# The first load of a streaming weighted sum: one DMA of 52 KB rows, and the last weights in three DMAs

## The chip, the core and the metric

The kernel runs on one core of one Trainium2 chip. The metric is device time in microseconds (us) of one execution. Before the change it is 238.91 us, the median of 3 runs (238.84 to 239.22).

## What is computed

For each of 16 x 1024 tokens there are two expert outputs of 512 floats and two weights. The result is their weighted sum.

```
batch, seq, hidden, k = 16, 1024, 512, 2
weights = combine_weights[..., np.newaxis]             # (16, 1024, 2, 1)
out = np.sum(expert_outputs * weights, axis=2)         # (16, 1024, 2, 512) -> (16, 1024, 512), float32
```

The input is 67 MB and the output is 33.5 MB. Two multiplications and one addition are done for each output element.

## The kernel before, in words

The 16384 tokens are dealt over 128 partitions, 128 tokens to each (`per`). The first 115 of a partition (`main`) lie together in memory, and the last 13 (`LAST`) lie together in a second region. A token is 4 KB of input (2 x 512 floats) and 2 KB of output. A partition's tokens are cut into ten tiles of 13, 13, 12, 13, 13, 13, 12, 13, 13 and 13 tokens (`TILES`), numbered 0 to 9. The buffer `et` has four rooms of 13, 13, 12 and 13 tokens, and tile g lives in room g mod 4. All weights fit in one buffer, `wt`.

`load` (line 76) moves a whole tile by one DMA on the queue of SyncE (SP in the profile, q1 among the DMA queues). Each partition's part of a tile is one row of the DMA: 13 tokens are 52 KB. Tile 0 is the exception: `FIRST` (line 33) splits it into a load of 2 tokens and one of 11, and line 119 tells the first that a row may not be longer than 4 KB, so it has 256 rows. Then come the loads of tiles 1, 2 and 3.

Ahead of the loads in the program, on the queue of ScalarE (ACT in the profile, q10 among the DMA queues), stand: a small store of zeros `zt` into places of the output that are written over later (line 111), the weights of the first 115 tokens of each partition (line 112, one DMA, 128 rows of 920 B), and those of the last 13 tokens in two DMAs of 64 partitions each (lines 113 and 114, rows of 104 B). The two engines issue side by side.

After that a loop runs over the stores (`STORES`). For tiles 0 to 7 `combine` does one multiplication of the whole tile by the weights on VectorE (DVE in the profile, line 88), in place, and one addition of the halves (line 97). Tile 8 shares its work with ACT (lines 92, 94, 96 and 97). Tile 9 goes token by token over ACT and DVE (lines 102 and 103). Its weights are the ones loaded last. The result lies in the tile's own room, and line 130 stores it: tiles 0 to 6 one at a time from ACT's queue, tiles 7 and 8 in one store and tile 9 in another from SP's queue. After the store of tile g, SP issues the load of tile g + 4 into the same room, which must wait until that store has landed. The program's order is the order on each engine's queue (`manual_schedule`); the waits between them are put in by the framework from what each instruction reads and writes. The framework also gives each DMA one of a few completion semaphores in turn, and a DMA that reuses one waits for the transfer that had it before.

Of the kernel before, what the change touches and what calls it, by code (L numbers as in the profile page):

```python
# [1 line left out]

# [4 lines left out]


@with_exitstack
def kernel(  # L10
    ctx: ExitStack,
    tc: tile.TileContext,
    expert_outputs: bass.AP,
    combine_weights: bass.AP,
    out: bass.AP,
):

    nc = tc.nc
    b, s, k, h = expert_outputs.shape
    assert k == 2
    n = b * s
    P = nc.NUM_PARTITIONS
    per = n // P
    assert per * P == n

    ROOM = [13, 13, 12, 13]
    ROOMS = len(ROOM)  # L30
    SITE = [sum(ROOM[:i]) for i in range(ROOMS)]
    TILES = [13, 13, 12, 13, 13, 13, 12, 13, 13, 13]
    FIRST = [2, 11, 13, 12, 13]
    STORES = [[0], [1], [2], [3], [4], [5], [6], [7, 8], [9]]
    WHOLE = [0, 1, 2, 3, 4, 5, 6, 7]
    MIXED = [8]
    ALONE = 3
    FREE = {9: 0}
    LAST = 13
    assert all(c <= ROOM[g % ROOMS] for g, c in enumerate(TILES))  # L40
    assert sum(TILES) == per and [g for st in STORES for g in st] == list(range(len(TILES)))
    main = per - LAST
    starts = [sum(TILES[:g]) for g in range(len(TILES))]

    def rows(x):

        first = x[0 : P * main, :].rearrange("(p t) f -> p t f", p=P)
        second = x[P * main : n, :].rearrange("(p t) f -> p t f", p=P)
        return lambda t, c: first[:, t : t + c, :] if t < main else second[:, t - main : t - main + c, :]

    flat = out.rearrange("b s h -> (b s) h")
    eo = rows(expert_outputs.rearrange("b s k h -> (b s) (k h)"))
    cw = rows(combine_weights.rearrange("b s k -> (b s) k"))
    o = rows(flat)

    dt = mybir.dt.float32
    mult = mybir.AluOpType.mult
    add = mybir.AluOpType.add
    copy = mybir.ActivationFunctionType.Copy

    pool = ctx.enter_context(tc.tile_pool(name="all", bufs=1))
    et = pool.tile([P, sum(ROOM), k * h], dt)
    halves = et.rearrange("p j (k h) -> p (j k) h", k=k)
    wt = pool.tile([P, per * k], dt)
    wk = wt.rearrange("p (t k) -> p t k", k=k)
    zt = pool.tile([16, 128], dt)
    warm = pool.tile([P, 1], dt)

    def place(t):
        g = max(g for g in range(len(TILES)) if starts[g] <= t)  # L70
        return SITE[g % ROOMS] + t - starts[g]

    def load(t, c, **kw):
        at = place(t)
        assert place(t + c - 1) == at + c - 1
        nc.sync.dma_start(out=et[:, at : at + c], in_=eo(t, c), **kw)  # L76

    def weights(q, t, c):
        q.dma_start(out=wk[:, t : t + c, :], in_=cw(t, c))

    def combine(g, base):
        at, c, t0 = SITE[g % ROOMS], TILES[g], starts[g]
        if g in WHOLE or g in MIXED:
            room = halves[:, k * at : k * (at + c), :]
            x0, x1 = et[:, at : at + c, 0:h], et[:, at : at + c, h : 2 * h]
            if g in WHOLE:
                wb = wt[:, k * t0 : k * (t0 + c)].unsqueeze(2).to_broadcast([P, k * c, h])
                nc.vector.tensor_tensor(out=room, in0=room, in1=wb, op=mult)  # L88
            else:
                for i in range(ALONE, c):  # L90
                    x = et[:, at + i, 0:h]
                    nc.scalar.activation(out=x, in_=x, func=copy, scale=wt[:, k * (t0 + i) : k * (t0 + i) + 1])  # L92
                w1 = wk[:, t0 : t0 + c, 1:2].to_broadcast([P, c, h])
                nc.vector.tensor_tensor(out=x1, in0=x1, in1=w1, op=mult)  # L94
                w0 = wk[:, t0 : t0 + ALONE, 0:1].to_broadcast([P, ALONE, h])
                nc.vector.tensor_tensor(out=x0[:, 0:ALONE], in0=x0[:, 0:ALONE], in1=w0, op=mult)  # L96
            nc.vector.tensor_tensor(out=halves[:, base : base + c, :], in0=x0, in1=x1, op=add)  # L97
            return
        for i in range(c):
            t = k * (t0 + i)  # L100
            x0, x1 = halves[:, k * (at + i), :], halves[:, k * (at + i) + 1, :]
            nc.scalar.activation(out=x0, in_=x0, func=copy, scale=wt[:, t : t + 1])  # L102
            nc.vector.scalar_tensor_tensor(  # L103
                out=halves[:, base + i, :], in0=x1, scalar=wt[:, t + 1 : t + 2], in1=x0, op0=mult, op1=add
            )

    with tc.manual_schedule():
        nc.vector.memset(zt, 0.0)  # L108

        ahead = flat[0 : P * main, :].rearrange("(q t) h -> q (t h)", q=16)  # L110
        nc.scalar.dma_start(out=ahead[:, 0:128], in_=zt)  # L111
        weights(nc.scalar, 0, main)
        for half in (slice(0, P // 2), slice(P // 2, P)):
            nc.scalar.dma_start(out=wk[half, main:per, :], in_=cw(main, per - main)[half])
        nc.scalar.activation(out=warm, in_=nc.const_aps.tensor(1.0, (P, 1), dt), func=copy)  # L115

        t = 0
        for i, c in enumerate(FIRST):
            load(t, c, **({"max_dma_last_dim": k * h * 4} if i == 0 else {}))
            t += c  # L120
        assert t == sum(TILES[:ROOMS])
        for j, st in enumerate(STORES):
            room = FREE.get(st[0], st[0] % ROOMS)
            base, c = SITE[room] * k, 0
            for g in st:
                combine(g, base + c)
                c += TILES[g]
            assert c <= k * ROOM[room]
            q = nc.sync if j in (7, 8) else nc.scalar
            q.dma_start(out=o(starts[st[0]], c), in_=halves[:, base : base + c, :])  # L130
            for g in st:
                if g + ROOMS < len(TILES):
                    load(starts[g + ROOMS], TILES[g + ROOMS])


# [1 line left out]
_INS = ['expert_outputs', 'combine_weights']  # L137
_OUTS = [((16, 1024, 512), 'float32')]


# [23 lines left out]
```

## Time and profile before

| | |
|---|---|
| median of 3 runs | 238.91 us |
| the profiled execution's own time | 238.91 us |
| its span, first to last instruction | 237.1 us |
| DVE busy | 190.0 us (80% of the span), 33 instructions |
| ACT busy | 15.8 us (7%), 25 instructions |
| DMA | 100.80 MB in 3344 packets, 425 GB/s over the span |
| first 2 tokens of tile 0, from issue to landing | 5.0 us |
| other 11 tokens of tile 0 | 18.2 us |
| weights of the first 115 tokens | 18.2 us |
| weights of the last 13 tokens | 31.0 us (median of two DMAs) |
| first multiplication on DVE starts at | 19.73 us |

How to read it: the span is cut at the first and the last instruction, and what lies outside it is part of the time alone. Instructions that issue DMAs are not counted as busy; they are listed with the time from issue to landing. In the view of DMA queues a packet is one row of a DMA, or a completion mark of 4 B, and the shares are those of the 16 DMA engines' time. In the timeline the bracket behind an instruction is the idle time of its engine ahead of it and what ended it.

### The profile page before, as it was taken

What the parts mean: (1) busy time and instruction counts of PE and PEld (TensorE: products, weight loads), DVE (VectorE), ACT (ScalarE), POOL (GpSimd) and SP (SyncE); (2) the same over time, 40 slices, a digit from 0 to 9 for tenths busy, and PEclk for the clock granted to TensorE, in tenths of its full rate; (3) what the DMA queues carried; (4) which work ended last, traced back from release to release, by engine and by line L of the source; (5) the groups of instructions that cost most, each with busy time, mean ns of one, the idle gap of its engine ahead of it and who ended that gap; (6) DMA issues with size and microseconds to landing.
All of it is one profiled execution on the core that took longest, in us unless ns stands there. A gap on an engine that the chain in (4) does not pass through costs nothing.

```text
span 237.1 us, 154 instructions
## 1 busy us (share of the span) xinstructions
DVE 190.0 (80%) x33; ACT 15.8 (7%) x25; POOL 0.2 (0%) x4
## 2 busy tenths in 40 slices
DVE  0006999999999999999999998998499969919400
ACT  2000000000000000000000000000000055019200
POOL 0000000000000000000000000000000000000000
DMA  8999999989999999999899999999899999899996
GB/s 300 388 481 434 432 421 398 470 348 485 449 431 458 431 440 390 486 420 420 359 492 409 409 509 392 431 503 431 359 431 503 420 397 483 381 431 431 431 431 287
DMA packets 3344, 100.80 MB, mean 425 GB/s; under 512 B 512, under 2 KB 656, under 8 KB 912
## 3 DMA queue, kind: packets, MB, share of 16 engines
q1 hardware_dynamic: 2000, 77.33, 75.9%
q10 hardware_dynamic: 1344, 23.47, 23.0%
HBM read 67.24 MB, written 33.56 MB: 425 GB/s over the span
## 4 chain that ended last, share of the span: by engine, by line
DVE 55%; DMA 36%; issue 1%; ACT 0%; DVEq 0%; ACTq 0%; SPq 0%
DVE et L88 35%; DVE et L97 17%; DMA out_dram<-et 17%; DMA et<-in_expert_outputs_dram 12%; DMA wt<-in_combine_weights_dram 8%; DVE et L103 3%; ACT et L102 0%; DVEq L159 0%; ACTq L111 0%; DVE zt L108 0%; DVEq L88 0%; SPq L76 0%; ACTq L102 0%
## 5 line engine op out<-in xcount | busy, mean ns | idle before, releaser
L88 DVE TENSOR_TENSOR et<-et,wt 128x13312 f32<-128x13312 f32 (+1 forms) x8 | 110.0, 13754 | 23.8 <-DMA wt<-in_combine_weights_dram 18.7
L97 DVE TENSOR_TENSOR et<-et 128x6656 f32<-128x6656 f32 (+1 forms) x9 | 62.8, 6973 | 0.4
L92 ACT ACTIVATE et<-et,wt 128x512 f32<-128x512 f32 x10 | 6.2, 708 | 188.0 <-DMA et<-in_expert_outputs_dram 188.0
L103 DVE SCALAR_TENSOR_TENSOR et<-et,wt 128x512 f32<-128x512 f32 x13 | 8.7, 747 | 5.0 <-ACT et L102 5.0
L102 ACT ACTIVATE et<-et,wt 128x512 f32<-128x512 f32 x13 | 8.1, 707 | 14.0 <-DMA et<-in_expert_outputs_dram 14.0
L94 DVE TENSOR_TENSOR et<-et,wt 128x6656 f32<-128x6656 f32 x1 | 7.1, 7093 | 2.3 <-DMA et<-in_expert_outputs_dram 2.3
L96 DVE TENSOR_TENSOR et<-et,wt 128x1536 f32<-128x1536 f32 x1 | 1.8, 1751 | 0.0
L115 ACT ACT_TABLE_LOAD x1 | 1.3, 1283 | 3.1 <-issue 3.1
L108 DVE MEMSET zt<- 16x128 f32 x1 | 0.2, 165 | 0.8 <-PEq L148 0.8
L115 ACT ACTIVATE warm<-const-float32-1.0 128x1 f32<-128x1 f32 x1 | 0.2, 203 | 0.0
L148 POOL MEMSET const-bfloat16-1.0<- 128x1 bf16 x1 | 0.1, 102 | 0.0
L148 POOL MEMSET const-uint8-127<- 128x1 uint8 x1 | 0.1, 101 | 0.0
L148 POOL MEMSET const-float32-0.0<- 128x1 f32 x1 | 0.1, 99 | 0.2 <-issue 0.2
L148 POOL MEMSET const-float32-1.0<- 128x1 f32 x1 | 0.1, 98 | 0.0
## 6 DMA issues: line engine op xcount, KB each, us to landing
et<-in_expert_outputs_dram SPq DMA_DIRECT2D x7, 6656.0 KB, 32.2
out_dram<-et ACTq DMA_DIRECT2D x5, 3328.0 KB, 34.7
et<-in_expert_outputs_dram SPq DMA_DIRECT2D x2, 6144.0 KB, 41.1
out_dram<-et SPq DMA_DIRECT2D x1, 6656.0 KB, 19.9
out_dram<-et ACTq DMA_DIRECT2D x2, 3072.0 KB, 37.2
et<-in_expert_outputs_dram SPq DMA_DIRECT2D x1, 5632.0 KB, 18.2
out_dram<-et SPq DMA_DIRECT2D x1, 3328.0 KB, 14.0
et<-in_expert_outputs_dram SPq DMA_DIRECT2D x1, 1024.0 KB, 5.0
```

The costliest lines, as they stand in the source:

```text
L88: nc.vector.tensor_tensor(out=room, in0=room, in1=wb, op=mult)
L92: nc.scalar.activation(out=x, in_=x, func=copy, scale=wt[:, k * (t0 + i) : k * (t0 + i) + 1])
L94: nc.vector.tensor_tensor(out=x1, in0=x1, in1=w1, op=mult)
L96: nc.vector.tensor_tensor(out=x0[:, 0:ALONE], in0=x0[:, 0:ALONE], in1=w0, op=mult)
L97: nc.vector.tensor_tensor(out=halves[:, base : base + c, :], in0=x0, in1=x1, op=add)
L102: nc.scalar.activation(out=x0, in_=x0, func=copy, scale=wt[:, t : t + 1])
L103: nc.vector.scalar_tensor_tensor(out=halves[:, base + i, :], in0=x1, scalar=wt[:, t + 1 : t + 2], in1=x0, op0=mult, op1=add)
L108: nc.vector.memset(zt, 0.0)
L115: nc.scalar.activation(out=warm, in_=nc.const_aps.tensor(1.0, (P, 1), dt), func=copy)
L148: nc = _bacc.Bacc("TRN2", target_bir_lowering=False, num_devices=1)
```

## The change

Tile 0 is loaded by one DMA of 13 tokens, with one row of 52 KB for each partition, like the tiles behind it. The weights of the last 13 tokens come in three DMAs of 48, 48 and 32 partitions in place of two of 64. The number of DMAs ahead of the first store stays nine.

```diff
-    FIRST = [2, 11, 13, 12, 13]
+    FIRST = [13, 13, 12, 13]
...
-        for half in (slice(0, P // 2), slice(P // 2, P)):
-            nc.scalar.dma_start(out=wk[half, main:per, :], in_=cw(main, per - main)[half])
+        for p in (slice(0, 48), slice(48, 96), slice(96, P)):
+            nc.scalar.dma_start(out=wk[p, main:per, :], in_=cw(main, per - main)[p])
...
-        for i, c in enumerate(FIRST):
-            load(t, c, **({"max_dma_last_dim": k * h * 4} if i == 0 else {}))
+        for c in FIRST:
+            load(t, c)
             t += c
```

## The prediction

> **What bounds the kernel now.** I read the page first: its span, the row of DMA shares and the two queues.
>
> ```profile
> span 237.1 us, 154 instructions
> DMA  8999999989999999999899999999899999899996
> q1 hardware_dynamic: 2000, 77.33, 75.9%
> q10 hardware_dynamic: 1344, 23.47, 23.0%
> ```
>
> The two queues together keep the 16 DMA engines busy for 75.9 + 23.0 = 98.9% of the span, 234.5 us. Only 2.6 us are left, nearly all ahead of the first packet and behind the last. DVE is busy 80%. So the end is set by moving 100.8 MB, and an edit can change the time in three ways: the packets take another time, the DMA engines start sooner or later, or they run dry somewhere in the middle. Next, a table by windows shows how the start goes.
>
> ```profile
> 0.00:1.80 1.80, 0.17 (x1) 0.00 (x0) 0.20 (x4) 1.00 0.00 0
> 62.00:212.00 150.00, 138.94 (x15) 6.23 (x10) 0.00 (x0) 1.00 1.00 433
> ```
>
> Its last two columns are DMA share and GB/s: nothing until 1.80 us, and 433 GB/s as the steady rate. The DMA view of 1.8 to 3.1 us shows the ramp, and that of 5.36 to 18.5 us how the two queues share:
>
> ```profile
> DMA packets 53, 0.22 MB, mean 167 GB/s; under 512 B 0, under 2 KB 0, under 8 KB 53
> ```
>
> ```profile
> DMA packets 224, 5.15 MB, mean 392 GB/s; under 512 B 0, under 2 KB 112, under 8 KB 112
> q1 hardware_dynamic: 112, 5.05, 88.7%
> q10 hardware_dynamic: 112, 0.10, 2.2%
> ```
>
> The ramp moves 167 in place of 433 GB/s for 1.3 us, a loss of 0.8 us. Then 112 rows of the load go with 112 rows of weights: each DMA engine takes one row from each queue by turns. A row of weights is short, but it waits for a long one. Last, the timeline, for who waits:
>
> ```profile
> 19.73 14.02 DVE L88 TENSOR_TENSOR et<-et,wt 128x13312 f32<-128x13312 f32 x1 [18.75 <-DMA wt<-in_combine_weights_dram]
> ...
> 145.69 12.96 DVE L88 TENSOR_TENSOR et<-et,wt 128x12288 f32<-128x12288 f32 x1 [1.10 <-DMA et<-in_expert_outputs_dram]
> ...
> 169.18 14.03 DVE L88 TENSOR_TENSOR et<-et,wt 128x13312 f32<-128x13312 f32 x1 [3.94 <-DMA et<-in_expert_outputs_dram]
> ...
> 192.63 7.09 DVE L94 TENSOR_TENSOR et<-et,wt 128x6656 f32<-128x6656 f32 x1 [2.30 <-DMA et<-in_expert_outputs_dram]
> ...
> 208.61 14.02 SPq L130 DMA_DIRECT2D out_dram<-et  x2
> ```
>
> DVE starts when the weights land (19.64 us), works without a pause for six tiles, and then waits for loads three times: 1.10 + 3.94 + 2.30 = 7.34 us of slack before the store at 208.61.
>
> **The change part by part.**
>
> *Rows of tile 0.* Each DMA engine serves 8 partitions. In the packet records a 4 KB row takes 0.156 us, one of 11 tokens 1.665 us and one of 13 tokens 1.966 us. Before: 16 x 0.156 + 8 x 1.665 = 15.82 us. After: 8 x 1.966 = 15.73 us. That is -0.09 us, on the path. A completion mark of 0.009 us goes from q1 and one comes to q10: nothing.
>
> *The ramp.* No row shows a 52 KB row as the first of all. If the wait for first data is paid once whatever the row, the 0.8 us stays; if it comes of many small rows, up to 0.8 us is gained. On the other side, the longest stretch of a long row in the trace is a 49152 B row at 43.5 us that took 2.46 in place of 1.815 us: up to +0.65. I take 0, since all 16 engines have their first 4 KB row by 2.1 us and most of those rows took 0.4 to 1.1 us, not 0.156: they waited for data, not for work.
>
> *The weights of the first 115 tokens.* They and `zt` are on q10 and now go by turns with 52 KB rows from the start. How soon does a row of q10 get its first turn? The nearest rows are those of the first store:
>
> ```profile
> q1 hardware_dynamic: 32, 1.57, 75.9%
> q10 hardware_dynamic: 16, 0.43, 18.6%
> issues: line engine op xcount, KB each, median us to landing
> out_dram<-et ACTq DMA_DIRECT2D x1, 3328.0 KB, 26.8
> ```
>
> This is the DMA view of 40.9 to 46.2 us. The store is issued at 40.91, and two more rows of the load start on each engine (32 over 16) before its own first row. So `zt`, issued at 1.01, goes after row 2 of tile 0 and its mark after row 3; rows 1 to 5 of the weights after rows 4 to 8; row 6 after tile 0's mark, which counts as a turn; rows 7 and 8 after rows 1 and 2 of tile 1; the weights' mark after row 3. Before, that mark came directly behind tile 0's last row, so the weights land three long rows later: 19.64 + 3 x 1.98 = 25.6 us. (With one turn gained, 23.6; if the weights were done with tile 0, 19.6.) Tile 0 itself lands at 19.4 as before. DVE starts near 25.7 in place of 19.73, 6 us late. What covers this: DVE needs 208.6 - 19.7 - 7.3 = 181.6 us of work up to the store of tiles 7 and 8, so it could issue that store at 25.7 + 181.6 = 207.3, still under 208.6, where the landing of tile 8 puts it now. The load of tile 9 feeds q1 until 212.1, and a first row needs 1.1 us from its issue (0.73 to 1.81 at the start), so the store must be issued by about 211.0. The slack is 3.7 us, nearly two rows.
>
> The Trainium skill, page "DMA: Bandwidth & Descriptors", section "Queues, rings and completion order", says that a DMA engine drains a packet of about 9 to 17 descriptors from one queue before it turns to the next. By that rule the 8 rows and the mark would go in one turn, DVE would wait for tile 0 alone and start at about 19.5; the end would be the same. The 112 against 112 rows speak against it.
>
> *What the late start moves.* Stores 0 to 5 are issued about 6 us late, and until the first of them q1 has the DMA engines alone, so the loads run ahead. The first store is issued near 46.9; its first row goes at about 51, not 45.75. Tile 3 is then in by about 72 (76.6 before) and the store of tile 0 lands at about 73.2 (67.75 before). The load of tile 4 waits for that landing: q1 is empty from about 71.7 to 74.5. But q10 holds the store of tile 1, issued by 67.9, and takes every turn meanwhile. Work is exchanged between the queues, none is lost. The same holds behind: the next stores land at about 93, 115 and 138, each issued at least 6 us before its predecessor lands. By tiles 6 to 8 DVE's 7.3 us of waiting have absorbed its 6 us. After the load of tile 9 the two last stores fill 228.1 - 212.1 = 16.0 and 8 us, and tile 9's store is issued 9.6 us after the load has landed, 4.5 us under cover still.
>
> A queue that comes back from empty may cost something. The nearest row is again the first store: the load rows next to it were stretched by 0.42 us per engine in all. Where q1 turns from loads to stores at 212.1 there is no stretch. Between 0 and 0.42 I take 0.2.
>
> *Three DMAs for the last weights.* The same 8 rows per engine, one mark and one turn more. One more issue of 0.51 to 0.61 us moves ACT's table load from 3.09 to 3.65; ACT next works at 192.6, so this is hidden. Counting turns, they land at about 44.2 (37.05 before). Tile 9 needs them at 212.8, but the first store takes over the completion semaphore of one of the first nine DMAs, and it stands behind this one if that is the last of the three: 44.2 is under 46.9, 2.7 us of cover. If that were gone, ACT's store would wait about 2 us for one turn, while q1 still has rows.
>
> The Trainium skill, same page, "Rules for kernel authors", advises one 128-partition transfer over two on disjoint partitions, and the section "Anatomy of one DMA" gives about 2.0 us as the fixed cost of a DMA. By that, the added one and the removed one cancel. No such cost shows between queued DMAs here: a row of tile 1 starts 0.01 us after tile 0's mark.
>
> *Sum.* -0.09 + 0 + 0.2 + 0 = +0.1 us on the profiled 238.91, which is also the median: 239.0. A difference of about 0.2%, 0.48 us, is what can be told from no change.
>
> **The rivals.**
>
> *A, the forecast, 0.50:* DVE starts 4 to 6 us late, the DMA engines stay busy, 238.5 to 239.3. *The change doesn't act, 0.03* (rows cut as before): 238.9.
>
> *B, DVE's slack is used up, 0.14, slower.* If the weights land more than 3.7 us later than I count (beyond about 29.3 us), the store of tiles 7 and 8 comes after q1 is empty, and each further turn costs 2.0 us at the end: two turns more cost 0.3 us, three 2.3, so 239.3 to 241.3. For it: each item on q10 costs one long row, and I have only one row for the first turn. Against it: that row shows two, not four or five.
>
> *C, the long first rows cost more, 0.16, slower.* The stretch of 0.65 at the ramp and 0.42 at the restart: -0.09 + 0.65 + 0.42 = +1.0, 239.9. For it: stretches occur at 43.5. Against it: the ramp before already holds a wait of 0.8.
>
> *D, the ramp gets shorter, 0.17, faster.* Long rows keep data flowing as soon as the first arrives: -0.09 - 0.8 + 0.2 = -0.7, 238.2. For it: 53 small rows needed 1.3 us. Against it: they had waited for data.
>
> **How the numbers follow.** The likeliest is A at 239.0, its own range 238.5 to 239.3. Same: 0.50 + 0.03 = 0.53, less 0.03 of A's upper edge given to slower, 0.50. Slower: 0.14 + 0.16 + 0.03 = 0.33. Faster: 0.17. The range takes in D's and C's times and the nearer half of B: 238.2 to 240.4; beyond it lie the outer parts of B and D, under 0.2.
>
> **What would show it.** In the changed profile: the weights' row at 24 us from issue in place of 18.2; the first multiplication at 25.7 (or 23.7 with one turn less); the three waits of DVE at tiles 6 to 8 nearly gone; the load of tile 4 issued near 73; the two queues' shares still summing to about 234 us. Wrong would be a DMA row with gaps in the middle or near 212 us (B), or first packets that end well away from 4.8 us (C, D).

## The result, and the profile after

The changed kernel takes 241.9 us, the median of 6 runs (240.73 to 243.55), against 238.88 us before (238.84 to 239.22). The ratio is 1.0126, with a 95% interval of 1.0099 to 1.0152: about 3 us slower, and spread over 2.8 us where the kernel before is spread over 0.4. The forecast was 239.0 us, no change, with a range up to 240.4.

The profiled execution is one of the quicker ones: 240.78 us, span 239.0. Page, in the order in which the page of before was read:

```profile
span 239.0 us, 153 instructions
...
DMA  7999999999999999899999999999999989989985
...
q1 hardware_dynamic: 1728, 77.33, 75.6%
q10 hardware_dynamic: 1360, 23.47, 23.0%
```

The kernel is as DMA-bound as before: 98.6% of 239.0 is 235.7 us of packet time, against 234.5. The same bytes took the average DMA engine 1.2 us longer. The span is 1.9 us longer, so something else is missing, and it is shown below. Timeline:

```profile
25.68 14.03 DVE L88 TENSOR_TENSOR et<-et,wt 128x13312 f32<-128x13312 f32 x1 [24.70 <-DMA wt<-in_combine_weights_dram]
...
173.00 14.03 DVE L88 TENSOR_TENSOR et<-et,wt 128x13312 f32<-128x13312 f32 x1 [3.00 <-DMA et<-in_expert_outputs_dram]
...
196.27 7.09 DVE L94 TENSOR_TENSOR et<-et,wt 128x6656 f32<-128x6656 f32 x1 [2.11 <-DMA et<-in_expert_outputs_dram]
...
212.25 12.23 SPq L130 DMA_DIRECT2D out_dram<-et  x2
```

DVE starts at 25.68 in place of 19.73, as counted. Of its three waits the first is gone, but those for tiles 7 and 8 are still 3.00 and 2.11 us: the loads are now late too (tile 8 at 196.2 us, 192.5 before), and the store of tiles 7 and 8 is issued 3.6 us later. The ramp and the sharing, in the DMA view of 1.7 to 2.8 us and that of 5.36 to 18.2:

```profile
q1 hardware_dynamic: 16, 0.85, 245.4%
```

```profile
q1 hardware_dynamic: 96, 5.11, 91.9%
q10 hardware_dynamic: 96, 0.07, 1.6%
```

The share counts the whole time of the packets that start in the window, so 245.4% of 1.1 us and 16 engines is 2.70 us for each first row, 0.73 more than the usual 1.966. The ramp costs the average engine what it cost before (0.8). Rows still go one for one. What is new lies later, in the DMA views of 74.3 to 78.6 us and of 78.6 to 79.9:

```profile
q10 hardware_dynamic: 65, 1.73, 98.1%
```

```profile
DMA packets 16, 0.85 MB, mean 655 GB/s; under 512 B 0, under 2 KB 0, under 8 KB 0
...
q1 hardware_dynamic: 16, 0.85, 198.0%
```

For 4.3 us only stores move, at full rate: the load queue is empty. Then each engine starts its first row of tile 4, and 198.0% of 1.3 us is 2.57 us a row, 0.61 over the usual. In the kernel before, the load queue never ran empty there, and its rows took 98.3% of 2.0 us, the usual 1.966 (view of 76.9 to 78.9 us):

```profile
q1 hardware_dynamic: 16, 0.85, 98.3%
```

The packet records name no engine, but a row starts within a few ns of the end of the one before it on its engine, so the sixteen can be followed one by one. In the changed kernel the second rows are stretched too, and some rows of the stores: 1.02 us per engine between 73 and 90 us, on average, and 0.59 to 1.9 from engine to engine. The last DMA view, 237.3 us to the end, is about the last engines:

```profile
q1 hardware_dynamic: 2, 0.00, 0.1%
```

Two completion marks are left alone at the end. Fourteen engines write theirs by 237.2 us, these two at 237.8. Before, all sixteen came within 0.32 us, the last at 235.97. The last store counts as landed with the last mark: 238.19, against 236.33.

### The profile page after: what moved, and what is told of

It is laid out like the page before. It is cut to its first block, busy times and chain, and to the rows that moved or that the text cites. A ratio compares the mean times of both kernels' runs of the same rounds, so it can differ in the third digit from the quotient of the medians.

```text
span 239.0 us, 153 instructions
## 1 busy us (share of the span) xinstructions
DVE 189.9 (79%) x33; ACT 15.8 (7%) x25; POOL 0.2 (0%) x4
## 4 chain that ended last, share of the span: by engine, by line
DVE 53%; DMA 37%; issue 3%; ACT 0%; DVEq 0%; ACTq 0%; SPq 0%
DVE et L88 35%; DVE et L97 15%; DMA out_dram<-et 14%; DMA et<-in_expert_outputs_dram 13%; DMA wt<-in_combine_weights_dram 10%; DVE et L103 3%; ACT et L102 0%; DVEq L159 0%; ACTq L111 0%; DVE zt L108 0%; SPq L76 0%; DVEq L88 0%; ACTq L102 0%
## 6 DMA issues: line engine op xcount, KB each, us to landing
wt<-in_combine_weights_dram ACTq DMA_DIRECT2D x1, 115.0 KB, 24.1
```

## The experiments

The theories were these, by the letters that the expectations use. **E**: DVE starts late, the store of tile 0 lands late, the load queue runs empty, and its restart costs the time. **L**: DVE's lateness itself costs it, through used-up slack. **R**: the 52 KB rows as the very first cost it at the start; later **S**: they leave one DMA engine behind. **W**: the third weights DMA does. **B2**: DMA engines idle before the late store of tiles 7 and 8.

### A late DVE by itself

The kernel before, with useless work ahead of tile 0 on DVE; loads and weights untouched. `N` is 11 in one kernel and 3 in the other.

```diff
+        x = et[:, 0:N, 0:h]
+        ones = nc.const_aps.tensor(1.0, (P, 1), dt).unsqueeze(2).to_broadcast([P, N, h])
+        nc.vector.tensor_tensor(out=x, in0=x, in1=ones, op=mult)
         for j, st in enumerate(STORES):
```

> The kernel before, with one extra multiplication by 1 of 11 half tokens on DVE ahead of tile 0, about 5.9 us, so that DVE starts near 25.5 us; loads and weights as before. Theory E: the store of tile 0 lands near 73 us, q1 is empty when the load of tile 4 is issued, rows near 80 us are stretched, 240.5 to 243.5 us. Theories R and W: 238.7 to 239.3 us, the time before, since no load or weights DMA is changed.

> The kernel before with DVE held by one multiplication by 1 of 3 half tokens, 1.6 us, so that it starts near 21.1 us, 1.4 us late. Theory E (a cost only from the point where the load queue runs empty, at about 2.3 us of lateness): 238.7 to 239.1 us. Theory L (each us of lateness costs its share, 1.97 us for 5.85): 239.3 to 239.5 us.

Measured: with 11, DVE starts tile 0 at 25.58 us and the kernel takes 240.83 us (240.44 to 241.11), ratio 1.0080 (1.0066 to 1.0094): +1.97 us. With 3, it starts at 21.04, 1.3 us late, and the kernel takes 238.90, ratio 1.0002 (0.9993 to 1.0010). The long hold shows the same empty queue and stretched rows (DMA views of 73.8 to 78.5 and of 78.5 to 79.9 us):

```profile
q10 hardware_dynamic: 74, 1.97, 100.9%
```

```profile
DMA packets 15, 0.80 MB, mean 571 GB/s; under 512 B 0, under 2 KB 0, under 8 KB 0
...
q1 hardware_dynamic: 15, 0.80, 176.4%
```

15 rows with 176.4% of 1.4 us and 16 engines are 2.63 us each. Between 73 and 90 us the packet records have 1.20 us of such stretch per engine on average, where the kernel before and the short hold have none. No engine idles before the store of tiles 7 and 8 (issued at 212.43, while the first engine ends tile 9's load at 213.3), so used-up slack at the end is not the cause here. So the late start is enough for two thirds of the loss without any change to loads or weights, and it costs nothing while the load queue still has rows. E holds against L, R and W for this part of the loss.

### The restart without a late DVE

The kernel before; the load of tile 4 is held by a small DMA into a buffer that DVE clears after the multiplication of tile 2.

```diff
                 nc.vector.tensor_tensor(out=room, in0=room, in1=wb, op=mult)
+                if g == 2:
+                    nc.vector.memset(gate, 0.0)
+                    nc.sync.dma_start(out=gate, in_=some[:, 0:128])
+                    load(starts[4], TILES[4])
+                    load(starts[5], TILES[5])
```

The first attempt left the load of tile 5 where it was, ahead of that of tile 4 on SP's queue:

> The kernel before, with the load of tile 4 held on SP by an 8 KB DMA that waits for the multiplication of tile 2 on DVE, to about 75 us; DVE itself starts at 19.7 as before. Theory E: q1 is empty from 76 to about 80 us while the store of tile 1 goes on, rows are stretched after that, about +1 to +3 us: 240 to 242 us. A rival of E (DVE's lateness and its used-up slack at tiles 7 and 8, not the empty queue): 238.7 to 239.5 us, since DVE has 7 us of slack here and work goes on in q10. R and W: 238.9 us.

It took 257.40 us, ratio 1.0788 (1.0765 to 1.0810). Tile 4's load stood behind tile 5's, which waits for a store until 81.5 us, and DVE had to wait for tile 4. This answers no question. The second attempt had the loads in order:

> The kernel before, with the load of tile 4 held on SP to about 75.5 us by an 8 KB DMA that waits for the multiplication of tile 2, and the load of tile 5 behind it in its usual order. DVE starts at 19.7 us as before. Theory E (the time is lost where the empty load queue starts again beside a running store): q1 is empty from 76 to about 79 us, the rows after that are stretched by about 1 us per DMA engine and more on the slowest, 240.0 to 242.0 us. Theory L (DVE's lateness itself, through the slack at tiles 7 and 8): 238.7 to 239.3 us, since DVE is not late.

It took 243.50 us (242.94 to 244.28), ratio 1.0196 (1.0179 to 1.0214), more than expected. DVE starts at 19.70 here, so lateness of DVE is not needed. The small DMA, issued at 74.93, moves its rows at about 78.8, and the load, issued at 75.39, at about 80.8; every later tile lands late, DVE waits 1.9 to 4.6 us for each of tiles 4 to 8, and the store of tiles 7 and 8 is issued at 216.65. The DMA view of 213.3 to 217.4 us:

```profile
DMA packets 18, 0.11 MB, mean 26 GB/s; under 512 B 16, under 2 KB 16, under 8 KB 16
...
q1 hardware_dynamic: 18, 0.11, 6.2%
```

Sixteen marks and two rows in 4.1 us: most engines stand idle, 3.5 us on average in the packet records, and rows are stretched again behind 90 us (1.20 us per engine). This is the prediction's rival B, reached through late loads. It is also why this run does not price the restart alone.

### The third weights DMA

Each part of the change alone: tile 0 in one load with the last weights in two DMAs, and the kernel before with the last weights in three.

> The changed kernel with the last weights in two DMAs of 64 partitions as before; tile 0 in one DMA of 52 KB rows. Theories E and R: like the changed kernel, 240.5 to 243.5 us, first multiplication at about 25.7 us. Theory W: 238.9 us.

> The kernel before with the last weights in three DMAs of 48, 48 and 32 partitions, and nothing else changed. Theory W (the third weights DMA costs time): 239.5 us or more. Theories E and R: 238.7 to 239.1 us, first multiplication at 19.7 us.

242.59 us (242.15 to 243.15), ratio 1.0149 (1.0133 to 1.0164), and 238.86 us, ratio 0.9997 (0.9989 to 1.0006). W falls: the three DMAs cost nothing, and the load of tile 0 carries the whole loss.

The profiled run of the two-weights kernel (243.15 us) shows what that of the changed kernel (240.78 us) does not. Fifteen engines write the mark of tile 0's store by 73.41 us, and one at 75.40; in the changed kernel the last came at 73.63. The store lands with that engine, so the load of tile 4 is issued at 76.04 in place of 74.25, and the store of tiles 7 and 8 at 213.60. The engines idle 1.2 us before it on average, and one ends 1.85 us behind the rest. Both kernels of the next section, which start as the changed kernel does, show the same late mark (75.16 and 75.47).

### The idle time at 213 us

The changed kernel with tiles 7 and 8 stored apart, so that the load queue always has a store behind tile 9's load.

```diff
-    STORES = [[0], [1], [2], [3], [4], [5], [6], [7, 8], [9]]
+    STORES = [[0], [1], [2], [3], [4], [5], [6], [7], [8], [9]]
...
-            q = nc.sync if j in (7, 8) else nc.scalar
+            q = nc.sync if j >= 7 else nc.scalar
```

> The changed kernel, with tile 7 stored by itself on SP's queue when it is ready, near 194 us, and tile 8 in a store of its own, in place of one store for both near 212 us. Theory B2 (part of the loss, and its spread from run to run, is that the DMA engines that finished tile 9's load first stand idle until the store of tiles 7 and 8 is issued): the idle at 213 us goes, the highest time falls from 243.5 to about 241, median 240.0 to 240.9 us. Theory E alone: the restart at 79 us stays and the median stays at 241 to 243 us.

It took 252.58 us, ratio 1.0575 (1.0562 to 1.0589), for a reason of its own: tile 9's result goes into room 0, where tile 8's store now still reads (DVE waited 19.16 us for it). With `FREE = {9: 2}` as well:

> The changed kernel with tiles 7 and 8 in two stores on SP's queue, the first issued near 194 us, and tile 9's result put into the room of tile 6, which is free by then. Theory B2 (a part of the loss and most of its spread is idle time of the DMA engines at 213 us, between the end of tile 9's load and the late store of tiles 7 and 8): no idle there, 240.2 to 241.0 us, highest under 241.5. Theory E alone (the restart, without such idle): 241 to 243.5 us as in the changed kernel.

242.36 us (242.30 to 242.96), ratio 1.0150 (1.0136 to 1.0163): not better than the changed kernel. The idle time is gone and 15 engines finish between 236.5 and 237.2 us, but the DMA view of 237.2 us to the end has this:

```profile
DMA packets 3, 0.05 MB, mean 14 GB/s; under 512 B 1, under 2 KB 1, under 8 KB 1
```

Two rows and a mark, of one engine, which ends at 240.05. B2 falls for this kernel: taking away the idle time of the engines that are early anyway gained nothing. What the program waits for is the one that is late. The Trainium skill's page "DMA: Bandwidth & Descriptors" says, in its section on the iDMA fabric, that a bulk load runs at the pace of its slowest engine. This trace agrees, for a store: 240.05 us against about 236.8 for the others.

### The long first rows by themselves

Three ways to keep the load of tile 0 and not the late DVE, or the reverse. First, the weights on SP's queue ahead of all loads, in the changed kernel and in the kernel before:

```diff
-        weights(nc.scalar, 0, main)
+        weights(nc.sync, 0, main)
```

> The changed kernel with the large weights DMA put on SP's queue ahead of the load of tile 0. Theory E (SP's load queue runs empty near 73 us because DVE starts late, and starting it again costs 1 to 2 us): the weights land early, DVE starts with tile 0 at about 19.8 us, the load of tile 4 is issued near 68 us while tile 3 still has rows, no stretched rows near 80 us, and the time is 238.6 to 239.4 us. Theory R (the 52 KB first rows cost by themselves at the start): 240.5 to 243.5 us as in the changed kernel. Theory W (the third weights DMA): 240.5 us or more too.

> The kernel before (tile 0 as 2 tokens in 4 KB rows and then 11) with the large weights DMA put on SP's queue ahead of it, as in the first experiment. It differs from that one in the first rows and in the two weights DMAs. Theory S (52 KB rows as the first put the DMA engines out of step, about +1.1 us): 238.6 to 239.2 us, the engines ending within 0.5 us. Its rival (the weights' place ahead of the loads cost the 1.46 us): 240.0 to 240.6 us.

240.32 us (239.59 to 240.57), ratio 1.0054 (1.0041 to 1.0066), with DVE at 20.64 and no empty queue: about half of the loss is back, which neither forecast had. But the kernel with short first rows took 240.17 us, ratio 1.0049 (1.0029 to 1.0069), with its runs in two groups, 239.0 to 239.6 and 240.7 to 241.0. The place of the weights costs something itself, so the pair says nothing for S.

Second, tile 0 in one load of 4 KB rows:

```diff
-            load(t, c)
+            load(t, c, **({"max_dma_last_dim": k * h * 4} if t == 0 else {}))
```

> The changed kernel, with tile 0 still in one DMA but its rows cut to 4 KB (1664 rows). The weights get their turns between short rows, so DVE starts with tile 0's landing, near 20 us. 104 rows of 0.156 us per DMA engine in place of 8 of 1.966: +0.5 us. Theories E and R: 239.0 to 239.8 us, no empty queue near 73 us. Theory W (the three weights DMAs): 241 us or more.

239.68 us (239.66 to 239.97), ratio 1.0038 (1.0026 to 1.0050), DVE at 20.83. Two thirds or more of the loss go with the long rows and the late DVE together, and by the row times 0.5 of the 0.8 us that stay are the shorter rows' own price. The runs are close together again.

Third, the work of tile 0 in two parts, so that the room comes free in two steps, in the changed kernel and in the kernel before:

```diff
+        for at, c in ((0, 7), (7, 6)):
+            part = halves[:, k * at : k * (at + c), :]
...
+            nc.scalar.dma_start(out=o(at, c), in_=res)
+            load(starts[4] + at, c)
```

> The changed kernel, with tile 0's multiplication, addition and store, and the load of tile 4 behind it, each in two parts of 7 and 6 tokens. The weights and DVE are as late as in the changed kernel (first multiplication at 25.7 us), but the first part of the load of tile 4 can be issued near 61 us, while tile 3 still has rows. Theory E: no stretched rows near 80 us; 238.8 to 240.0 us. Theory L, and theory R (52 KB rows at the start): 241 to 243 us as in the changed kernel.

> The kernel before with tile 0's work, its store and the load of tile 4 in two parts of 7 and 6 tokens; DVE on time, short first rows. Control of the changed kernel in two parts, which took 239.95 us. Theory S: 238.7 to 239.1 us, so that those 1.1 us belong to the long first rows. If it takes about 239.9 us too, the two parts cost that by themselves.

239.95 us (239.52 to 240.88), ratio 1.0059 (1.0043 to 1.0075), with DVE at 25.71 and no stretched rows near 80 us: with the queue kept full, a start 6 us late costs at most 1.1 us. In the kernel before, the two parts took 240.08 us, ratio 1.0064 (1.0039 to 1.0090): its store of tiles 7 and 8 is issued at 212.41, and the engines idle 0.7 to 1.2 us. So the 1.1 us can't be put down to the long rows from this pair either.

The pair that tells most: the weights on SP's queue behind tile 0, in both kernels. The two also differ in the last weights' DMAs, three and two, which cost nothing in the kernel before (0.9997).

```diff
+            if t == 13:
+                weights(nc.sync, 0, main)
```

> The changed kernel with the large weights DMA on SP's queue behind the load of tile 0, so that it doesn't wait for turns. Tile 0 comes in 52 KB rows as the very first, DVE starts near 20.2 us, the load queue doesn't run empty. Theory S (the long first rows leave a DMA engine behind, and that costs about 1.1 us at the end): 239.6 to 240.6 us, the last engine's load of tile 9 ending 1 us or more behind the first. Its rival (the whole loss comes of the late DVE): 238.7 to 239.2 us.

> The kernel before with the large weights DMA on SP's queue behind the two loads of tile 0: like the run beside it, but with 2 tokens in 4 KB rows first. Both theories: 238.7 to 239.2 us. If it is slower, the weights' place costs something, and only the difference of the two kernels speaks on the first rows.

Long first rows, DVE at 20.11: 240.84 us, ratio 1.0069 (1.0050 to 1.0089); the six runs are 239.43, 240.03, 240.74, 240.93, 240.96 and 241.20. Short first rows, DVE at 19.87: 238.94 us, ratio 1.0009 (0.9988 to 1.0031); ten of twelve runs lie between 238.81 and 239.04, and two at 240.88. In the profiled run of each, both of them near 241 us, the view of 236.3 us to the end is the same line:

```profile
DMA packets 2, 0.03 MB, mean 10 GB/s; under 512 B 1, under 2 KB 1, under 8 KB 1
```

One engine has a row and a mark left, 1.7 to 1.9 us after the next slowest (237.81 against 236.16, and 237.95 against 236.04). So the extra 2 us in such a run are one engine that has fallen behind by one long row. By the times of the runs it can happen with short first rows (2 runs of 12, and 1 of the 18 runs of the kernel before on that chip, at 240.88). With long ones it happened in at least 4 of 6.

The packet records show where it falls behind, and it is not at the first rows. Between 44 and 71 us, where the first stores move beside the loads, the rows of the late engine took 2.0 us (long first rows) and 2.2 us (short) longer in sum than such rows usually take, those of any other engine at most 0.75; after 73 us nothing is stretched. In the run with tile 7 stored apart it was 2.2 us against at most 0.8. So S holds only in a weaker form: with long first rows a straggler was seen more often. That rests on these counts and on the two intervals, which don't overlap; how the first rows bring about a lag 40 us later is not shown.

## Why the prediction was wrong

**Right.** The counting of turns: the weights landed after 24.1 us in the queue, the first multiplication started at 25.68 (25.7 said), the first store was issued at 46.86 (46.9), the last weights landed at 44.6 (44.2), the load of tile 4 was issued at 74.25 (73.2). The ramp's mean cost stayed (though by 2.1 us 14 engines of the kernel before had their first row, not all 16), rows of tile 0 cost nothing, and the third weights DMA cost nothing (0.9997). Rival D, a shorter ramp, did not come. Rival C put +0.65 us into the ramp, where 0.05 was found (0.75 against 0.70 us of stretch per engine), and +0.42 into the restart: the right place for that part, and too little.

**Wrong: the price of a queue that comes back from empty.** This term was put between 0 and 0.42 us and taken at 0.2. It measured 1.02 us per engine on average in the changed kernel. The nearest row, the first store at 43.5 us, was the right kind of event and the wrong size. The late DVE that causes the restart costs 1.97 us in all when it is made alone.

**Wrong: the sum was made for an average engine.** "Work is exchanged between the queues, none is lost" holds for the sixteen together, the stretch above apart. A transfer lands with its last engine. The stretches fall unevenly (0.59 to 1.9 us at the restart), so the last engine lies 1.0 us behind the median one at the end of the profiled run, and 3.2 us behind in the run with tile 7 stored apart. A late engine also acts earlier: tile 0's store lands with it, and with a mark 2 us late the load of tile 4 is issued at 76.0 in place of 74.25. The spread of 2.8 us over the runs fits this: the two lowest (240.73 and 240.78) took what the late DVE alone took (240.83), and the profiled runs with the late mark took 242.96 and 243.15 (the third, 252.62, has a wait of its own). The other runs of the changed kernel itself have no trace, so this is not shown for them. Long first rows add a late engine without a restart too (240.84 against 238.94 us). No step of the prediction asked how far the engines are apart, though the marks in the trace of before would have shown that they ended within 0.32 us.

**Wrong: 1.1 us to a first row.** That came from the very first load, with idle DMA engines. Load 4 was issued at 74.25 and moved at 78.66, 4.4 us later. The nearer row was in the prediction: the first store, issued at 40.91 beside a busy queue, moved its first row at 45.75, 4.8 us later. It was used for the stores and not for this load. The queue was empty about twice as long as foreseen (72.65 to 78.66, not 71.7 to 74.5), and the later loads landed 3.6 us late in place of slightly early. DVE's waits for tiles 7 and 8 therefore stayed.

**Rival B** named the right place, the store of tiles 7 and 8. In the profiled run it came at 212.25, and the engines that ended tile 9's load first idled 0.4 us at most, 0.1 on average over the sixteen. In the two-weights run the average was 1.2. Taking the idle time away gained nothing (242.36 us). In the kernel with load 4 held, B became the larger part of the loss.

The parts don't add up exactly: late DVE alone +1.97, long first rows alone +1.96 by the medians, together +3.0 (+3.7 with two weights DMAs). By their times, the runs with long first rows are a mixture, some with a late engine and some without. Why one engine is hit more than the others, and why rows are stretched at all when a queue starts beside a busy one, stays open; no run here changes that alone. In the profiled runs with the late mark a large part of the stretch comes not at the load's first rows but at 88 to 91 us (0.54 to 0.65 us per engine), just ahead of the first rows of tile 2's store, so the load queue's return is not the only place where it falls. None of the kernels tried was faster than the one before.

## What to carry to other kernels

Where transfers are the bound, conservation of bytes is not enough for a forecast: ask which queue runs empty, what its restart costs, and how far apart the DMA engines are when they finish, since every wait is for the last of them. A short row queued beside long ones costs a long row per turn, so what the first instruction needs should not share turns with the bulk load. A late engine is free only up to the point where a queue behind it runs dry; find that point (here between 1.3 and 5.9 us of lateness) before calling slack a cover. And one trace need not hold what sets the median: that of the changed kernel has no mark 2 us late, those of three kernels that start like it have one.

## What the runs showed of the hardware that was not expected

- A load issued while another queue kept the DMA engines busy moved its first row 4.4 us after its issue (74.25 to 78.66); with the engines idle it took 1.0 us (0.73 to 1.73).
- When the load queue started again beside a running store, 53248 B rows that take 1.966 us took 2.57 us on average.
- One DMA engine of sixteen can end a whole row behind, and then the kernel takes about 240.9 in place of 238.9 us: by the times, 1 run of 18 of the kernel before, 4 or more of 6 with 52 KB rows first. In three traced runs it fell behind between 44 and 71 us, where two queues shared the engines, by 2.0 to 2.2 us, and never caught up.
- Weights issued on the load queue ahead of all loads made the kernel slower (1.0049, 1.0029 to 1.0069) although DVE started at 19.97 us; behind tile 0 they cost nothing that shows (1.0009, 0.9988 to 1.0031).
